# Eight experts on one core: five output stores move from the SyncE queue into GpSimd's queue of loads

## The chip, the core and the metric

The kernel runs on one core of one Trainium2 chip. The metric is the device time of one execution in microseconds (us); before the change the median of five runs is 186.20 us (185.97 to 186.28). The profile used here is one execution of 186.28 us, whose first to last instruction span 184.3 us.

## What is computed

Eight experts, each a two-layer network with its own weights, each on its own 256 rows. All inputs and the output are float32 in device memory.

```python
# n_experts 8, capacity 256, hidden 512, expert_hidden 2048
# x (8,256,512)  w1 (8,512,2048)  w2 (8,2048,512)  b1 (8,2048)  b2 (8,512)
h = np.matmul(x, w1) + b1[:, np.newaxis, :]
h = np.maximum(h, 0)
return (np.matmul(h, w2) + b2[:, np.newaxis, :]).astype(np.float32)
```

The weights are 67.1 MB of the 71.4 MB that the program reads; the output is 4.2 MB.

## The kernel before the change

**Tiles.** Rows of a 128-partition tile are interleaved with the free dimension, so that each partition reads one contiguous run of device memory. The loads issued by GpSimd convert float32 to float16 on the way: `w1sb` and `w2sb` are 128 x 8192 float16 tiles of 2048 KB, `x16` is 256 KB. There are three buffers for w1, three for w2, four for x. The last two w2 are cut: expert 6 comes in two halves (L82), and expert 7 in six pieces with buffers of their own (L90): j 0-4, 4-8, 8-12 (512 KB each), 12-14 (256 KB), and 14-16 in two column halves (128 KB each). They are called p0 to p5 below.

**Stages.** TensorE's work is written out in order. Stage s holds `first_product(s)` (16 values of j, each four matmuls into PSUM at L110 and one relu with bias on ScalarE at L117) and, from s = 3 (LAG), `second_product(s - 3)`: the bias b2 by a one-row matmul (L151), then for every piece of w2, both row blocks and every j one matmul (L163). In the middle of `first_product(e)`, after j = 8, stand the eight transposes of the x of expert e + 1 (L97) with the copy of the result by VectorE (L103). So expert e + 1's x holds up TensorE if it is late, and everything written behind it.

**Stores.** At the end of `second_product(e)`, `store` copies the two PSUM row blocks into an `out` tile, one on VectorE (L130) and one on ScalarE (L131). For experts 0 to 6 one DMA of 512 KB, 4096 bytes to a partition, goes out on SyncE's queue (L137), which has nothing else to do then. For expert 7 each column half is stored in two DMAs of 128 KB, one on SyncE (L134) and one on ScalarE (L135). The `out` tiles have two buffers.

**The order of the loads.** Nearly all loads are GpSimd DMAs and leave in one order: w1(0), b2, w1(1), x(2), w1(2), x(3), w1(3), w2(0), x(4), w1(4), w2(1), x(5), w1(5), w2(2), x(6), w1(6), w2(3), x(7), w1(7), w2(4), w2(5), the halves of w2(6), p0 to p5. `load_x`, `load_w1` and `load_w2` are entries of a list; `issue_until` issues them ahead of the stage that needs them. GpSimd works in order: where a load waits for its buffer (w1(6) for the end of `first_product(3)`, w2(5) for the end of `second_product(2)`), the loads behind it wait too. In the built program a GpSimd DMA also waits for the eighth GpSimd DMA before it, since eight semaphores are used in turn. All DMAs of this queue are called the ring in what follows; the profile names it q0, software_dynamic. SyncE's queue is q1, ScalarE's q10, both hardware_dynamic.

Of the kernel before, what the change touches and what calls it, by code (L numbers as in the profile page):

```python
# [11 lines left out]
def kernel(  # L12
# [9 lines left out]
    nc = tc.nc  # L22
    fp32 = mybir.dt.float32
    fp16 = mybir.dt.float16
    E, T, H = x.shape
    M = w1.shape[2]
    P = 128
    nTB = T // P
    nKC = H // P
    nJ = M // P  # L30
    HH = H // 2
    LAG = 3
    nXF32 = 2

    def ordered(ins):
        return tc.keep_in_program_order(ins)

    singles = ctx.enter_context(tc.tile_pool(name="singles", bufs=1))
    w1_pool = ctx.enter_context(tc.tile_pool(name="w1", bufs=3))
    w2_pool = ctx.enter_context(tc.tile_pool(name="w2", bufs=3))  # L40
    w2t_pool = ctx.enter_context(tc.tile_pool(name="w2t", bufs=1))
    x_pool = ctx.enter_context(tc.tile_pool(name="xp", bufs=4))
    xT_pool = ctx.enter_context(tc.tile_pool(name="xTp", bufs=2))
    hT_pool = ctx.enter_context(tc.tile_pool(name="hT", bufs=LAG + 2))
    out_pool = ctx.enter_context(tc.tile_pool(name="outp", bufs=2))
    psum_x = ctx.enter_context(tc.tile_pool(name="psum_x", bufs=1, space=bass.MemoryType.PSUM))
    psum_h = ctx.enter_context(tc.tile_pool(name="psum_h", bufs=3, space=bass.MemoryType.PSUM))
    psum_o = ctx.enter_context(tc.tile_pool(name="psum_o", bufs=2, space=bass.MemoryType.PSUM))
# [10 lines left out]
    w1_sb = [None] * E  # L59
    w2_sb = [None] * E  # L60
    hT = [None] * E

    def load_x(e):
        x16[e] = x_pool.tile([P, nTB, H], fp16, tag="x16", name="x16")
        ordered(nc.gpsimd.dma_start(  # L65
            out=x16[e], in_=x[e].rearrange("(p tb) h -> p tb h", tb=nTB)
        ))
# [7 lines left out]
    def load_w2(e):  # L75
        src = w2[e].rearrange("(p j) h -> p j h", j=nJ)
        w2_sb[e] = []
        if e < E - 1:
            t = w2_pool.tile([P, nJ, H], fp16, tag="w2", name="w2sb")
            step = nJ if e < E - 2 else nJ // 2  # L80
            for lo in range(0, nJ, step):
                ordered(nc.gpsimd.dma_start(out=t[:, lo : lo + step, :], in_=src[:, lo : lo + step, :]))  # L82
                w2_sb[e].append((lo, lo + step, 0, H, t[:, lo : lo + step, :]))
            return
        for lo, hi, c0, c1 in (
            (0, 4, 0, H), (4, 8, 0, H), (8, 12, 0, H), (12, 14, 0, H),
            (14, 16, 0, HH), (14, 16, HH, H),
        ):
            t = w2t_pool.tile([P, hi - lo, c1 - c0], fp16, tag=f"w2_{lo}_{c0}", name=f"w2_{lo}_{c0}")
            ordered(nc.gpsimd.dma_start(out=t, in_=src[:, lo:hi, c0:c1]))  # L90
            w2_sb[e].append((lo, hi, c0, c1, t))

    def transposes(e):
        pt = psum_x.tile([P, nKC, T], fp16, tag="psx", name="psx")
        for kc in range(nKC):
            for tb in range(nTB):
                ordered(nc.tensor.transpose(  # L97
                    out=pt[:, kc, tb * P : (tb + 1) * P],
                    in_=x16[e][:, tb, :].rearrange("p (q kc) -> p q kc", kc=nKC)[:, :, kc],
                    identity=ident16,  # L100
                ))
        xT[e] = xT_pool.tile([P, nKC, T], fp16, tag="xT", name="xT")
        nc.vector.tensor_copy(out=xT[e], in_=pt)  # L103

    def first_product(e):
        hT[e] = hT_pool.tile([P, nJ, T], fp16, tag="hT", name="hT")
        for j in range(nJ):
            ph = psum_h.tile([P, T], fp32, tag="ph", name="ph")
            for kc in range(nKC):
                ordered(nc.tensor.matmul(  # L110
                    out=ph,
                    lhsT=w1_sb[e][:, kc, :].rearrange("p (q j) -> p q j", j=nJ)[:, :, j],
                    rhs=xT[e][:, kc, :],
                    start=(kc == 0),
                    stop=(kc == nKC - 1),
                ))
            nc.scalar.activation(  # L117
                out=hT[e][:, j, :],
                in_=ph,
                func=mybir.ActivationFunctionType.Relu,  # L120
                bias=b1T[:, j, e : e + 1],
                scale=1.0,
            )
            if j == nJ // 2 and e + 1 < E:
                transposes(e + 1)

    def store(e, po, c0, c1, split):
        w = c1 - c0
        out_sb = out_pool.tile([P, nTB, w], fp32, tag=f"out{w}", name=f"out{w}")
        nc.vector.tensor_copy(out=out_sb[:, 0, :], in_=po[0])  # L130
        nc.scalar.copy(out=out_sb[:, 1, :], in_=po[1])  # L131
        dst = out[e].rearrange("(p tb) h -> p tb h", tb=nTB)[:, :, c0:c1]
        if split:
            nc.sync.dma_start(out=dst[:, 0, :], in_=out_sb[:, 0, :])  # L134
            nc.scalar.dma_start(out=dst[:, 1, :], in_=out_sb[:, 1, :])  # L135
        else:
            nc.sync.dma_start(out=dst, in_=out_sb)  # L137

    def second_product(e):
        if e < E - 1:  # L140
            blocks = [(0, H, psum_o, "po")]
        else:
            blocks = [(0, HH, psum_o, "po"), (HH, H, psum_h, "ph")]
        acc = {}
        for c0, c1, pool, tag in blocks:
            for tb in range(nTB):
                t = pool.tile(
                    [P, c1 - c0], fp32, tag=tag if tag == "ph" else f"{tag}{tb}", name=f"acc{tb}"
                )
                acc[c0, tb] = t  # L150
                ordered(nc.tensor.matmul(  # L151
                    out=t,
                    lhsT=ones1,
                    rhs=b2_sb[0:1, e * H + c0 : e * H + c1],
                    start=True,
                    stop=False,
                ))
        for lo, hi, p0, p1, t in w2_sb[e]:
            mine = [b for b in blocks if p0 <= b[0] and b[1] <= p1]
            for tb in range(nTB):  # L160
                for j in range(lo, hi):
                    for c0, c1, _, _ in mine:
                        ordered(nc.tensor.matmul(  # L163
                            out=acc[c0, tb],
                            lhsT=hT[e][:, j, tb * P : (tb + 1) * P],
                            rhs=t[:, j - lo, c0 - p0 : c1 - p0],
                            start=False,
                            stop=(j == nJ - 1),
                        ))
            if hi == nJ:  # L170
                for c0, c1, _, _ in mine:
                    store(e, [acc[c0, tb] for tb in range(nTB)], c0, c1, e == E - 1)

    x32 = singles.tile([P, nXF32, nTB, H], fp32)
    for e in range(nXF32):
# [4 lines left out]
        out=b2_sb,  # L180
        in_=b2.rearrange("e h -> (e h)").rearrange("(o f) -> o f", o=1),
# [10 lines left out]
    for j in range(nJ):  # L192
        for s in range(2):
            ordered(nc.tensor.matmul(  # L194
                out=pb[s * 64 : (s + 1) * 64, j, :, :],
# [5 lines left out]
    for s in range(2):  # L201
        nc.vector.tensor_copy(  # L202
            out=b1T[s * 64 : (s + 1) * 64, :, :], in_=pb[s * 64 : (s + 1) * 64, :, :, s]
        )
    transposes(0)

    loads = []
    for s in range(1, E + LAG):
        if s < E:
            if s >= nXF32:  # L210
                loads.append((load_x, s))
            loads.append((load_w1, s))
        if s >= LAG:
            loads.append((load_w2, s - LAG))
    n = 0

    def issue_until(done):
        nonlocal n
        while n < len(loads) and not done():
            loads[n][0](loads[n][1])  # L220
            n += 1

    for s in range(E + LAG):
        issue_until(lambda: (
            (min(s + 2, E - 1) < E and w1_sb[min(s + 2, E - 1)] is not None)
            and (s + 2 < LAG or w2_sb[min(s + 2 - LAG, E - 1)] is not None)
        ))
        if s < E:
            first_product(s)
        if s >= LAG:  # L230
            second_product(s - LAG)


# [28 lines left out]
```

## Time and profile before

| | |
|---|---|
| median of five runs | 186.20 us |
| profiled execution | 186.28 us, its span 184.3 us, granted TensorE clock 0.926 |
| TensorE matmul busy | 137.9 us (75%) |
| ScalarE busy | 62.7 us (34%) |
| VectorE / GpSimd busy | 13.5 us / 16.9 us |
| bytes | 71.39 MB read, 4.19 MB written, 410 GB/s over the span |
| stores of experts 0 to 6 | 7 issues, median 9.0 us from issue to landing |
| the same, last two (experts 5 and 6) | issued at 164.0 and 172.0 us, landed 8.1 and 6.6 us later |

How to read it: the span is cut into slices with each engine's busy share in tenths; the DMA row is the mean of the 16 DMA engines. The queues are listed with bytes and with the share of 16 engines' time that their packets took; a load counts there with the float16 bytes that it writes, so its megabytes are half of what it reads. The timeline lists instructions of an engine in order, with the idle time before a group and what ended it. The chain of waits is followed back from the last instruction to what released it.

### The profile page before, as it was taken

The page shows a single profiled execution, that of the slowest core. Times are in us where ns is not written, and L with a number is a line of the kernel's source. Part 1 is how long each engine was busy: PE and PEld are TensorE (multiplying, and loading weights), DVE is VectorE, ACT ScalarE, POOL GpSimd, SP SyncE. Part 2 cuts the span into 40 slices and gives each one's busy share as a digit, 9 for nine tenths or more (in the row PEclk, how much of TensorE's full clock was granted, in tenths as well). Part 3 has the DMA queues.
Part 4 walks back from the last instruction along what each step waited for, and adds up shares of the span by engine and source line. Part 5 has one row for each costly group of instructions (what it writes and reads, how often), then busy time and mean ns, then how long its engine had stood idle before and what let it go on. Part 6 is the DMA issues. An engine that isn't in the chain of part 4 may idle for free.

```text
span 184.3 us, 2209 instructions
## 1 busy us (share of the span) xinstructions
PE 137.9 (75%) x946; PEld 99.1 (54%) x946; DVE 13.5 (7%) x22; ACT 62.7 (34%) x138; POOL 16.9 (9%) x37
## 2 busy tenths in 40 slices
PE   0546969396561999529995499916999996999971
PEld 0534969296551846428465364815648842434750
DVE  0320101001000100001010101001010010101001
ACT  0022869487260513604226060631506901010101
POOL 7100030302100012000110000100006200100000
PEclk9999999999875699965999789995799999999999
DMA  5999999999999999999999999999999999999983
GB/s 198 271 213 194 220 228 224 198 204 229 228 224 199 203 228 228 180 275 220 206 199 243 264 211 217 203 272 232 206 203 224 238 251 206 244 235 254 218 199 114
DMA packets 6488, 40.57 MB, mean 220 GB/s; under 512 B 688, under 2 KB 1728, under 8 KB 4432
## 3 DMA queue, kind: packets, MB, share of 16 engines
q0 software_dynamic: 4320, 35.14, 91.2%
q1 hardware_dynamic: 1568, 4.46, 6.5%
q10 hardware_dynamic: 592, 0.85, 1.3%
q8 instruction: 7, 0.11, 0.2%
q14 instruction: 1, 0.01, 0.0%
HBM read 71.39 MB, written 4.19 MB: 410 GB/s over the span
## 4 chain that ended last, share of the span: by engine, by line
DMA 57%; PE 31%; another core or an unknown queue 5%; POOL 3%; issue 1%; ACT 0%; ACTq 0%; POOLq 0%
DMA x<-in_x_dram 25%; DMA w<-in_w_dram 19%; PE ph L110 16%; DMA w1sb<-in_w_dram 12%; PE acc L163 12%; PE psx L97 2%; PE acc L151 1%; POOL w2sb L82 1%; POOL w L90 1%; POOL w1sb L71 1%; ACT out L131 0%; POOL b_sb L179 0%; POOL ident masks.py:199 0%; ACTq L135 0%
## 5 line engine op out<-in xcount | busy, mean ns | idle before, releaser
L110 PE MATMUL ph<-xT,w1sb 128*128 128x256 f16 x512 | 68.6, 300 | 11.7 <-DMA w1sb<-in_w_dram 11.7
L117 ACT ACTIVATE hT<-ph,b1T 128x256 f16<-128x256 f32 x128 | 57.0, 473 | 47.6 <-PE ph L110 47.5
L110 PEld LDWEIGHTS <-w1sb 128*128 128x128 f16 x512 | 61.8, 149 | 17.9 <-DMA w1sb<-in_w_dram 12.7
L163 PE MATMUL acc<-w2sb,hT 128*128 128x512 f16 x224 | 49.7, 379 | 1.8 <-DMA w2sb<-in_w_dram 1.8
L163 PEld LDWEIGHTS <-hT 128*128 128x128 f16 x288 | 27.5, 98 | 32.2 <-issue 6.8
L131 ACT COPY out<-acc 128x512 f32<-128x512 f32 (+1 forms) x9 | 4.9, 541 | 59.9 <-PE acc L163 59.9
L97 PE MATMUL psx<-ident,x 128*128 128x128 f16 x64 | 7.0, 276 | 21.3 <-DMA x<-in_x_dram 20.6
L97 PEld LDWEIGHTS <-x 128*128 128x128 f16 x64 | 5.6, 132 | 22.3 <-DMA x<-in_x_dram 21.5
L103 DVE COPY xT<-psx 128x1024 f16<-128x1024 f16 x8 | 5.5, 691 | 85.1 <-PE psx L97 85.1
L130 DVE COPY out<-acc 128x512 f32<-128x512 f32 (+1 forms) x9 | 5.7, 632 | 73.5 <-PE acc L163 73.5
L71 POOL DMA_DIRECT2D w1sb<-in_w_dram x8 | 4.4, 553 | 68.0 <-PE ph L110 67.2
L82 POOL DMA_DIRECT2D w2sb<-in_w_dram x8 | 4.3, 536 | 57.1 <-PE acc L163 57.1
L194 PE MATMUL pb<-ident,b_rows 16*64 16x16 f32 x64 | 3.7, 266 | 6.5 <-DMA b_rows<-in_b_dram 6.5
L163 PE MATMUL acc<-w,hT 128*128 128x256 f16 x64 | 7.5, 272 | 1.2 <-DMA w<-in_w_dram 1.2
L194 PEld LDWEIGHTS pb<-ident,b_rows 16*64 16x64 f32 x64 | 3.6, 198 | 6.5 <-issue 6.5
L117 ACT ACT_TABLE_LOAD x1 | 1.3, 1283 | 10.9 <-DVE b1T L202 10.9
L151 PE MATMUL acc<-b_sb,ones 1*128 1x512 f16 (+1 forms) x18 | 4.8, 355 | 0.0
L90 POOL DMA_DIRECT2D w<-in_w_dram x6 | 3.6, 613 | 12.6 <-DMA w2sb<-in_w_dram 12.6
L65 POOL DMA_DIRECT2D x<-in_x_dram x6 | 3.3, 546 | 2.3 <-DMA w1sb<-in_w_dram 2.3
L151 PEld LDWEIGHTS <-ones 1*128 1x128 f16 x18 | 1.1, 93 | 2.1 <-issue 2.1
L189 DVE CAST x<-x 128x1024 f16<-128x1024 f32 x2 | 1.5, 764 | 4.2 <-DMA x<-in_x_dram 4.1
L202 DVE COPY b1T<-pb 64x128 f32<-64x128 f32 x2 | 0.6, 288 | 3.5 <-PE pb L194 3.5
(8 smaller groups left out, 2.0 us busy)
## 6 DMA issues: line engine op xcount, KB each, us to landing
w1sb<-in_w_dram POOLq DMA_DIRECT2D x8, 2048.0 KB, 33.6
w2sb<-in_w_dram POOLq DMA_DIRECT2D x6, 2048.0 KB, 47.3
out_dram<-out SPq DMA_DIRECT2D x7, 512.0 KB, 9.0
w2sb<-in_w_dram POOLq DMA_DIRECT2D x2, 1024.0 KB, 24.5
x<-in_x_dram POOLq DMA_DIRECT2D x6, 256.0 KB, 40.3
w<-in_w_dram POOLq DMA_DIRECT2D x3, 512.0 KB, 32.0
x<-in_x_dram ACTq DMA_DIRECT2D x1, 512.0 KB, 5.3
x<-in_x_dram SPq DMA_DIRECT2D x1, 512.0 KB, 4.4
```

Of the source, the lines that this page charges most:

```text
L71: ordered(nc.gpsimd.dma_start(out=w1_sb[e], in_=w1[e].rearrange("(p kc) m -> p kc m", kc=nKC)))
L82: ordered(nc.gpsimd.dma_start(out=t[:, lo : lo + step, :], in_=src[:, lo : lo + step, :]))
L90: ordered(nc.gpsimd.dma_start(out=t, in_=src[:, lo:hi, c0:c1]))
L97: ordered(nc.tensor.transpose(out=pt[:, kc, tb * P : (tb + 1) * P], in_=x16[e][:, tb, :].rearrange("p (q kc) -> p q kc", kc=nKC)[:, :, kc] ...
L103: nc.vector.tensor_copy(out=xT[e], in_=pt)
L110: ordered(nc.tensor.matmul(out=ph, lhsT=w1_sb[e][:, kc, :].rearrange("p (q j) -> p q j", j=nJ)[:, :, j], rhs=xT[e][:, kc, :], start=(kc == 0),
L117: nc.scalar.activation(out=hT[e][:, j, :], in_=ph, func=mybir.ActivationFunctionType.Relu, bias=b1T[:, j, e : e + 1], scale=1.0,)
L130: nc.vector.tensor_copy(out=out_sb[:, 0, :], in_=po[0])
L131: nc.scalar.copy(out=out_sb[:, 1, :], in_=po[1])
L151: ordered(nc.tensor.matmul(out=t, lhsT=ones1, rhs=b2_sb[0:1, e * H + c0 : e * H + c1], start=True, stop=False,))
L163: ordered(nc.tensor.matmul(out=acc[c0, tb], lhsT=hT[e][:, j, tb * P : (tb + 1) * P], rhs=t[:, j - lo, c0 - p0 : c1 - p0], start=False, sto ...
L194: ordered(nc.tensor.matmul(out=pb[s * 64 : (s + 1) * 64, j, :, :], lhsT=b1_rows.rearrange("r (q j) -> r q j", j=nJ)[:, :, j], rhs=ident[0 ...
```

## The change

Experts 0 to 4 no longer store on SyncE's queue. `store` puts the DMA by (`pending`), and `flush` issues it on GpSimd, at a set place in the list of loads, which now carries the earliest stage with each entry: flush(0) stands behind w2(3), flush(1) behind w2(4), flush(2) behind w2(5), flush(3) behind the halves of w2(6), and flush(4) between p0 and p1. Experts 5 and 6 still store on SyncE, expert 7 on SyncE and ScalarE. The `out` tiles of 512 columns have three buffers where they had two, and the two of expert 7 have their own. The loads keep their order among themselves, and TensorE, VectorE and ScalarE keep theirs. In the built program GpSimd issues 34 DMAs where it issued 29, and SyncE four stores where it issued nine.

```diff
+    RING = 4
-    out_pool = ctx.enter_context(tc.tile_pool(name="outp", bufs=2))
+    out_pool = ctx.enter_context(tc.tile_pool(name="outp", bufs=3))
+    pending = {}
...
-        for lo, hi, c0, c1 in (
-            (0, 4, 0, H), (4, 8, 0, H), (8, 12, 0, H), (12, 14, 0, H),
-            (14, 16, 0, HH), (14, 16, HH, H),
-        ):
-            t = w2t_pool.tile([P, hi - lo, c1 - c0], fp16, tag=f"w2_{lo}_{c0}", name=f"w2_{lo}_{c0}")
-            ordered(nc.gpsimd.dma_start(out=t, in_=src[:, lo:hi, c0:c1]))
-            w2_sb[e].append((lo, hi, c0, c1, t))
+    def load_w2_piece(e, lo, hi, c0, c1):
+        t = w2t_pool.tile([P, hi - lo, c1 - c0], fp16, tag=f"w2_{lo}_{c0}", name=f"w2_{lo}_{c0}")
+        src = w2[e].rearrange("(p j) h -> p j h", j=nJ)
+        ordered(nc.gpsimd.dma_start(out=t, in_=src[:, lo:hi, c0:c1]))
...
+    def flush(e):
+        dst, src = pending.pop(e)
+        ordered(nc.gpsimd.dma_start(out=dst, in_=src))
+
     def store(e, po, c0, c1, split):
         w = c1 - c0
-        out_sb = out_pool.tile([P, nTB, w], fp32, tag=f"out{w}", name=f"out{w}")
+        pool = out_pool if w == H else singles
+        out_sb = pool.tile([P, nTB, w], fp32, tag=f"out{c0}_{w}", name=f"out{w}")
...
+        elif e <= RING:
+            pending[e] = (dst, out_sb)
         else:
             nc.sync.dma_start(out=dst, in_=out_sb)
...
+    ring = []
+    for s in range(1, E + LAG - 1):
         if s < E:
             if s >= nXF32:
-                loads.append((load_x, s))
-            loads.append((load_w1, s))
+                ring.append((s - 2, load_x, (s,)))
+            ring.append((s - 2, load_w1, (s,)))
         if s >= LAG:
-            loads.append((load_w2, s - LAG))
...
+            ring.append((s - 2, load_w2, (s - LAG,)))
+        if s >= 2 * LAG:
+            ring.append((s - 2, flush, (s - 2 * LAG,)))
+    e = E - LAG - 1
+    for piece in (
+        (0, 4, 0, H), (4, 8, 0, H), (8, 12, 0, H), (12, 14, 0, H),
+        (14, 16, 0, HH), (14, 16, HH, H),
+    ):
+        ring.append((0, load_w2_piece, (E - 1,) + piece))
+        if e <= RING:
+            ring.append((e + LAG + 1, flush, (e,)))
+            e += 1
 
     for s in range(E + LAG):
...
+        while ring and ring[0][0] <= s:
+            _, put, args = ring.pop(0)
+            put(*args)
```

More of the change, by code (lines that the diff above doesn't have):

```diff
@@ L77, in load_w2 @@
         w2_sb[e] = []
[L78 to L84, printed above, removed]
-        for lo, hi, c0, c1 in (
-            (0, 4, 0, H), (4, 8, 0, H), (8, 12, 0, H), (12, 14, 0, H),
-            (14, 16, 0, HH), (14, 16, HH, H),
-        ):
-            t = w2t_pool.tile([P, hi - lo, c1 - c0], fp16, tag=f"w2_{lo}_{c0}", name=f"w2_{lo}_{c0}")
-            ordered(nc.gpsimd.dma_start(out=t, in_=src[:, lo:hi, c0:c1]))
-            w2_sb[e].append((lo, hi, c0, c1, t))
+        t = w2_pool.tile([P, nJ, H], fp16, tag="w2", name="w2sb")
+        step = nJ if e < E - 2 else nJ // 2
+        for lo in range(0, nJ, step):
+            ordered(nc.gpsimd.dma_start(out=t[:, lo : lo + step, :], in_=src[:, lo : lo + step, :]))
+            w2_sb[e].append((lo, lo + step, 0, H, t[:, lo : lo + step, :]))
+    def load_w2_piece(e, lo, hi, c0, c1):
+        t = w2t_pool.tile([P, hi - lo, c1 - c0], fp16, tag=f"w2_{lo}_{c0}", name=f"w2_{lo}_{c0}")
+        src = w2[e].rearrange("(p j) h -> p j h", j=nJ)
+        ordered(nc.gpsimd.dma_start(out=t, in_=src[:, lo:hi, c0:c1]))
+        if w2_sb[e] is None:
+            w2_sb[e] = []
+        w2_sb[e].append((lo, hi, c0, c1, t))
     def transposes(e):
@@ L205 @@
     transposes(0)
-    loads = []
-    for s in range(1, E + LAG):
+    ring = []
+    for s in range(1, E + LAG - 1):
         if s < E:
             if s >= nXF32:
-                loads.append((load_x, s))
-            loads.append((load_w1, s))
+                ring.append((s - 2, load_x, (s,)))
+            ring.append((s - 2, load_w1, (s,)))
         if s >= LAG:
-            loads.append((load_w2, s - LAG))
[L215 to L221, printed above, removed]
+            ring.append((s - 2, load_w2, (s - LAG,)))
[10 more added lines that the diff above has]
+            e += 1
     for s in range(E + LAG):
[L224 to L227, printed above, removed]
+        while ring and ring[0][0] <= s:
+            _, put, args = ring.pop(0)
+            put(*args)
         if s < E:
@@ L231 @@
             second_product(s - LAG)
+    assert not ring and not pending
 _INS = ['x', 'w1', 'w2', 'b1', 'b2']
```

## The prediction

> **What bounds the kernel now.** I read the slices of the page and its list of queues first, then TensorE's timeline, the chain of waits, and the DMA queues in windows.
>
> ```profile
> DMA  5999999999999999999999999999999999999983
> ...
> q0 software_dynamic: 4320, 35.14, 91.2%
> q1 hardware_dynamic: 1568, 4.46, 6.5%
> ```
>
> The DMA engines are nine tenths busy or more from the second slice (of 4.6 us) to the 38th, q0 (the ring) with 91.2% of their time, SyncE's queue with 6.5%. No stretch is empty that a load could be pulled into. TensorE is fed by the ring; its timeline, each row with start, time, and idle time before it:
>
> ```profile
> 26.09 4.15 PE L110 MATMUL ph<-xT,w1sb 128*128 128x256 f16 x36 [1.40 <-DMA w1sb<-in_w_dram]
> ...
> 37.01 4.15 PE L110 MATMUL ph<-xT,w1sb 128*128 128x256 f16 x36 [3.26 <-DMA w1sb<-in_w_dram]
> ...
> 58.99 1.04 PE L97 MATMUL psx<-ident,x 128*128 128x128 f16 x8 [5.09 <-DMA x<-in_x_dram]
> ...
> 81.97 1.04 PE L97 MATMUL psx<-ident,x 128*128 128x128 f16 x8 [5.93 <-DMA x<-in_x_dram]
> ...
> 103.91 1.04 PE L97 MATMUL psx<-ident,x 128*128 128x128 f16 x8 [4.44 <-DMA x<-in_x_dram]
> ...
> 125.85 1.04 PE L97 MATMUL psx<-ident,x 128*128 128x128 f16 x8 [5.15 <-DMA x<-in_x_dram]
> ...
> 156.22 7.07 PE L163 MATMUL acc<-w2sb,hT 128*128 128x512 f16 x32 [1.49 <-DMA w2sb<-in_w_dram]
> ...
> 167.67 3.61 PE L163 MATMUL acc<-w2sb,hT 128*128 128x512 f16 x16 [0.29 <-DMA w2sb<-in_w_dram]
> ...
> 176.15 1.91 PE L163 MATMUL acc<-w,hT 128*128 128x256 f16 x16 [0.73 <-DMA w<-in_w_dram]
> 178.53 1.94 PE L163 MATMUL acc<-w,hT 128*128 128x256 f16 x16 [0.47 <-DMA w<-in_w_dram]
> ```
>
> A row that waits for a DMA dates that DMA's landing. The last two rows are p2 (16 matmuls) and p3 to p5 (8, 4, 4). The chain of waits ends:
>
> ```profile
> 142.56 35.93 DMA w<-in_w_dram
> 178.48 0.04 issue
> 178.53 1.48 PE acc L163 x12
> 180.01 0.02 issue
> 180.03 0.38 ACT out L131
> ```
>
> So p3's landing at 178.48 sets the end, then 12 matmuls, then ScalarE and the last stores, 184.3 − 180.01 = 4.3 us, which the change leaves alone.
>
> **Two prices.** Between 26.09 and 37.01 the ring brought one w1 and one x, 2304 KB in 10.92 us: 211 KB per us. So 512 KB (p0, p1, p2 each) takes 2.43 us, 256 KB (p3) 1.21. From x(5) to x(6), 81.97 to 103.91, and from x(6) to x(7), 103.91 to 125.85, are 21.94 us each; a w1, a w2 and an x are 4352 KB or 20.63 us; the 1.31 left over is one store. From x(4) to x(5), 58.99 to 81.97, it is 22.98, so the first store cost 2.35. The window 72 to 82 gives that store 13.8% of 10 us, 1.38 us of packets; the other 1 us is load packets that ran slow, once.
>
> **The change, part by part.**
> *Bytes.* None are added or removed. Before, all seven stores pass ahead of p3's landing; after, five stand ahead of p3 in the ring, and the two of SyncE come earlier than now. If a store costs the ring what it costs beside it, p3 lands at 178.48 again: 0 us.
>
> *The price of a ring store* is not shown. The nearest rows are 1.31 and 2.35 for one on SyncE's queue, 1.21 for 256 KB of x in the ring, whose float32 bytes are a store's, 512 KB. Bounds: 0 (it hides wholly) makes 5 x −1.31 = −6.6 us, 2.35 each makes 5 x 1.04 = +5.2. I take 1.31, by the two regular stores and the near 1.21; at 1.21 it would be −0.5. Three rows lie within 0.1 of each other, so neither far end is in the range. The single excess of 1 us I let recur, at the first ring store or the first SyncE store; if it stays away, −1.0.
>
> The Trainium skill ("DMA: Bandwidth & Descriptors", Anatomy of one DMA) gives a GpSimd DMA a fixed cost of about 2.0 us, most of it the receipt of the last write, worst to device memory. Charged to the ring five times, an estimate by that page, it would be +10 us. The row that bears on it: the ring's 29 DMAs run with the DMA engines at nine tenths throughout, so that cost lies beside other packets in this trace, though no store is among them.
>
> *Instructions on GpSimd.* Five more issues of 0.55 us (the row of x loads: 3.3 us for 6), beside waits of 67.2 us (w1) and 57.1 us (w2): nothing, for the loads behind them wait 20 to 50 us in the ring. Of their waits, flush(0) to flush(3) follow w2 loads that already wait for the `second_product` that makes the output. For flush(0): w2(3) issued at 72.41, the output is ready at 72.74. New is flush(4): GpSimd reaches it at about 140, expert 4's output is ready at about 152, and p1 to p5 wait behind it. The ring then still holds flush(2), w2(6), flush(3), p0 and flush(4), 1.3 + 9.7 + 1.3 + 2.4 + 1.3 = 16 us: hidden, while that output is less than 16 us late. The wait for the eighth DMA back makes p5 follow w2(6)'s second half (165) with p0 to p4 and two stores, some 12 us, in front: hidden too. If not, each us of empty ring is 1 us of time.
>
> *Third buffer.* out(6) waits for flush(3), which follows w2(6) in the ring (about 165.1 + 1.3 + 1.3 for a SyncE store between, 167.7); ScalarE needs it at about 168.7. One us of cover; without it only store 6 is late, which costs nothing.
>
> *What comes sooner.* The stores are later, so the loads are earlier. Ahead of w2(5) lay stores 0 to 3, now flush(0) and flush(1): two fewer, 2.6 us, so landing 153.6 for 156.2. Ahead of w2(6)'s end lay 0 to 4, now flush(0) to flush(2): 165.1 for 167.67. x(7) comes at 123.2 for 125.85, and TensorE's work to 154.2 shifts with it. So TensorE ends `second_product(6)` 2.6 us earlier, and SyncE issues store 6 at 169.4 instead of 172.0. The loads after that give the 2.6 us back: flush(3) and flush(4) now stand before p1.
>
> *The tail.* Where did store 6 go before? The window 175 to 178.5:
>
> ```profile
> q0 software_dynamic: 493, 0.34, 64.3%
> q1 hardware_dynamic: 144, 0.52, 39.7%
> ```
>
> All its 0.52 MB, 1.39 us of packets, ran there, 3.0 us after its issue, and so between the landings of p2 and p3: 178.48 − 176.1 is 2.4 us, where p3 alone takes 1.21. This gap let TensorE finish p2 (1.91 us) with 0.47 to spare. After, store 6 runs from 169.4 + 3.0 = 172.4 to about 176, beside p1 and the first part of p2. p3 still lands at 178.48, by the sum of bytes, but p2 then lands 1.21 before it, at 177.27, not at 176.1. TensorE starts p2 at 177.32, ends at 179.23, and does the 12 matmuls behind it without a wait: 179.23 + 1.48 = 180.71 for 180.01. **+0.70 us**: TensorE, not p3, is then the last to wait for.
>
> The Trainium skill (same page, "Issuing engines are not separate DMA queues") says that moving a DMA to another queue saves only issue time, since all run on the same 16 engines; that alone would make 0, 186.3 us. For the bytes the row of slices agrees; the order at the tail is what it leaves out.
>
> **Sum.** 186.28 + 0.70 = 186.98 for an execution like the profiled one; this stood 0.08 above the median of the runs, so 186.9.
>
> **Rivals.**
> 1. *Nothing moves* (186.2, 185.8 to 186.5). Store 6 still falls between p2 and p3. For: stores on SyncE's queue took 8 to 15 us to land in the middle of the run. Against: the last two took 8.1 and 6.6, and 169.4 + 8.1 is 177.5. It decides when half the store, 0.6 us, lies behind p2.
> 2. *Faster* (185.4, 184.4 to 185.8). Ring stores are cheaper than SyncE's: the slow load packets at the first store do not recur (−1.0), or each store costs 1.21 (−0.5); with the +0.7 of the tail, 186.2 − 1.5 + 0.7 = 185.4. The hope that earlier loads alone end earlier is worth at most TensorE's waits of 1.49 and 0.29, to 184.4, but p3's landing speaks against it. For: the 2.35 beside 1.31. Against: the later stores showed no such excess, so there is at most one to save.
> 3. *Much slower* (188.5 to 195). A store in the ring holds the loads behind it until its write is confirmed. The last 128 KB stores took 2.1 us from issue to landing, and their bytes take 0.3: 1.8 x 5 = 9.0, +0.7 = 195.9 if all of it holds the ring; a quarter makes 188.9. For: such a wait would be beside the ring before, inside it after. Against: no gap behind any load in the slices. It decides from a hold of 0.1 us per store.
>
> **How the numbers follow.** My forecast 0.47, rival 1 0.25, rival 2 0.20, rival 3 0.08. About 0.2%, 0.37 us, is what can be told from no change: 185.8 to 186.6. Faster 0.20 is rival 2; the same 0.25 is rival 1; slower 0.55 is my forecast and rival 3. The likeliest case alone spans 186.5 to 187.4 (half of store 6 behind p2 to one more excess of a half us); the range takes in rival 1 and the edge of rivals 2 and 3: 185.7 to 187.8.
>
> **What would show it.** Right: in TensorE's timeline the matmuls of `second_product(5)` start near 153.6, p2 near 177.3, and p3 to p5 follow without a wait for a DMA; store 6 is issued near 169.4; the queue shares keep 98% in sum; the chain ends in more matmuls than 12. Wrong: p3 waits for a DMA again (rival 1), p3 lands under 178 (rival 2), slices under nine tenths or a store's share in the ring above 1.4 us (rival 3). An idle DMA engine between 141 and 170 would say that flush(4) starved the ring.

## The result, and the profile after

Median 186.30 us over 23 runs (186.12 to 187.06) beside 186.04 us over 44 runs of the kernel before: ratio 1.0022, 95% interval 1.0015 to 1.0029. The change costs 0.3 us by the medians and 0.4 by the ratio; the forecast was a cost of 0.7. The 23 runs fall into two groups, 14 from 186.12 to 186.36 and 9 from 186.58 to 187.06; those of the kernel before show no such gap. The profiled execution took 186.30 us, its span is 184.5 us.

From the page of the changed kernel, the slices of the DMA engines and the queues:

```profile
DMA  5998999999999999998999989999999999999973
...
q0 software_dynamic: 5040, 37.76, 94.6%
q1 hardware_dynamic: 848, 1.84, 2.8%
```

Five stores of 0.52 MB have gone from q1 to q0; the packet time of the two is 97.4% of the span where it was 97.7%. No stretch has run empty. TensorE's timeline in the changed kernel (start, time, in brackets the idle time before the row and what ended it):

```profile
122.93 1.04 PE L98 MATMUL psx<-ident,x 128*128 128x128 f16 x8 [7.33 <-DMA x<-in_x_dram]
...
153.22 8.75 PE L171 MATMUL acc<-w2sb,hT 128*128 128x512 f16 x32 [2.19 <-DMA w2sb<-in_w_dram]
...
172.90 1.91 PE L171 MATMUL acc<-w,hT 128*128 128x256 f16 x16 [0.99 <-DMA w<-in_w_dram]
176.03 3.82 PE L171 MATMUL acc<-w,hT 128*128 128x256 f16 x32 [1.22 <-DMA w<-in_w_dram]
```

x(7) comes at 122.93 for 125.85, w2(5) at 153.2 for 156.2. The last row holds p2 to p5 in one: TensorE waits for p2 and for nothing behind it. The chain of waits says the same, with 28 matmuls behind the DMA of p2 where 12 stood behind p3:

```profile
153.46 22.53 DMA w<-in_w_dram
175.99 0.04 issue
176.03 3.35 PE acc L171 x28
179.38 0.02 issue
179.40 0.38 ACT out L137
```

But ScalarE's copy starts at 179.40, 0.63 us *earlier* than before (180.03), and the span is 0.2 us longer. What is lost lies behind it, where no engine computes. Two views show it. In them a drain is one of an engine's closing instructions, and a slot is one of the eight semaphores that the DMAs of SyncE and ScalarE use in turn. SyncE's own waits at the end, first of the kernel before, then of the changed one (total, times, longest):

```profile
SPq L257 <- DMA out_dram<-out: 1.9, 4, 1.0
```

```profile
SPq L271 <- DMA out_dram<-out: 2.1, 1, 2.1
```

Before the program ends, SyncE waits for the semaphores of all DMA queues, two to an instruction, in a fixed order of slots. Before, four of these waits were spread over the landings; after, the wait for the first slot holds until the last landing and the others follow it. And the end itself, before and after (operation, count, durations, first and last start):

```profile
L257 SPq DRAIN  x3: 7/7/7, 183.5 to 183.8; - x3
...
L257 POOLq EVENT_SEMAPHORE_RANGE_CLEAR  x1: 141/141/141, 183.9 to 183.9; - x1
```

```profile
L271 SPq DRAIN  x3: 7/7/7, 183.2 to 183.5; - x3
...
L271 POOLq EVENT_SEMAPHORE_RANGE_CLEAR  x1: 139/139/139, 184.1 to 184.1; - x1
```

SyncE's drain, which says that all DMAs are done, comes 0.3 us earlier than before, and GpSimd's clearing of the semaphores 0.2 us later: GpSimd's own drain ahead of it starts at 183.81, 0.45 us after the wait before it, where it was 0.08 us. In that last stretch the changed kernel has one packet on the instruction queue, the kernel before none (queues in the window 183 to 186: packets, MB, share):

```profile
q14 instruction: 1, 0.01, 1.0%
```

It starts at 184.52, where the span ends, 0.7 us behind that drain.

The table gathers what the semaphore and packet records of every profile give; us from the span's start. SyncE's drain is the second of its three, 0.06 us behind the first, and the last column runs from its start to the end of the execution (device time less that start).

| kernel | p2 | p3 | p5 | ScalarE's first store | last landing | SyncE's drain | to the end |
|---|---|---|---|---|---|---|---|
| before | 176.11 | 178.48 | 179.82 | 180.43 | 183.30 | 183.56 | 2.72 |
| changed | 175.99 | 177.85 | 179.21 | 179.81 | 182.67 | 183.25 | 3.05 |
| changed, again | 176.51 | 177.77 | 179.12 | 180.21 | 183.07 | 183.65 | 3.04 |
| before, 3 tiny loads | 175.79 | 177.27 | 179.71 | 180.15 | 183.03 | 183.60 | 2.72 |
| changed, 7 tiny loads | 175.98 | 177.71 | 179.01 | 179.67 | 182.54 | 182.68 | 3.07 |
| before, 5 tiny ring loads | 175.81 | 177.54 | 179.72 | 180.14 | 183.05 | 183.31 | 3.04 |
| changed, store 4 behind p2 | 174.97 | 177.72 | 179.07 | 179.67 | 182.53 | 183.11 | 3.04 |
| before, 16 memsets | 175.53 | 177.02 | 179.45 | 179.89 | 182.75 | 183.01 | 2.54 |
| changed, 16 memsets | 175.97 | 177.83 | 179.19 | 179.79 | 182.65 | 183.22 | 2.54 |
| changed, all three edits | 175.21 | 178.00 | 179.31 | 179.95 | 182.82 | 182.96 | 2.54 |
| three buffers alone | 176.17 | 178.38 | 179.69 | 180.34 | 183.20 | 183.46 | 2.71 |
| 5 and 6 behind p5 | 174.07 | 175.30 | 176.70 | 177.77 | 180.66 | 180.80 | 2.58 |
| 4, 5 and 6 behind p5 | 172.80 | 174.01 | 175.45 | 176.50 | 180.55 | 180.69 | 2.58 |
| 0 to 4 on SyncE, 5 and 6 behind p5 | 174.32 | 175.53 | 176.97 | 178.21 | 181.08 | 181.46 | 2.93 |

From the first two rows: −0.62 to ScalarE's store, +0.31 from there to SyncE's drain (3.13 to 3.44), +0.33 behind it: +0.02, as the two executions differ (186.28, 186.30). What this pair hides is said under "Sum".

### The profile page after: what moved, and what is told of

The parts are those of the page before. It is cut to its first block, busy times and chain, and to the rows that moved or that the text cites. A ratio compares the mean times of both kernels' runs of the same rounds, so it can differ in the third digit from the quotient of the medians.

```text
span 184.5 us, 2204 instructions
## 1 busy us (share of the span) xinstructions
PE 138.4 (75%) x946; PEld 98.8 (54%) x946; DVE 13.4 (7%) x22; ACT 62.7 (34%) x138; POOL 19.6 (11%) x42
## 4 chain that ended last, share of the span: by engine, by line
DMA 71%; PE 14%; issue 8%; another core or an unknown queue 2%; POOL 2%; ACT 0%; ACTq 0%; POOLq 0%
DMA x<-in_x_dram 24%; DMA w2sb<-in_w_dram 22%; DMA w1sb<-in_w_dram 12%; DMA w<-in_w_dram 12%; PE ph L111 7%; PE acc L171 6%; PE psx L98 1%; POOL w2sb L83 1%; POOL w1sb L73 1%; ACT out L137 0%; POOL out_dram L130 0%; PE acc L159 0%; POOL b_sb L187 0%; POOL ident masks.py:199 0%
## 5 line engine op out<-in xcount | busy, mean ns | idle before, releaser
L111 PE MATMUL ph<-xT,w1sb 128*128 128x256 f16 x512 | 67.8, 298 | 8.8 <-DMA w1sb<-in_w_dram 8.8
L171 PE MATMUL acc<-w2sb,hT 128*128 128x512 f16 x224 | 51.2, 389 | 2.2 <-DMA w2sb<-in_w_dram 2.2
L171 PEld LDWEIGHTS <-hT 128*128 128x128 f16 x288 | 28.0, 99 | 34.8 <-issue 10.2
L130 POOL DMA_DIRECT2D out_dram<-out x5 | 2.7, 538 | 18.3 <-ACT out L137 13.1
```

Of the source, the lines that this page charges most:

```text
L111: ordered(nc.tensor.matmul(out=ph, lhsT=w1_sb[e][:, kc, :].rearrange("p (q j) -> p q j", j=nJ)[:, :, j], rhs=xT[e][:, kc, :], start=(kc == 0),
L171: ordered(nc.tensor.matmul(out=acc[c0, tb], lhsT=hT[e][:, j, tb * P : (tb + 1) * P], rhs=t[:, j - lo, c0 - p0 : c1 - p0], start=False, sto ...
```

## The experiments

Each was timed beside the kernel before on the same chip. "Tiny" loads are 64 bytes that nothing reads.

**The changed kernel once more**, for a second profile.

> The changed kernel once more, for a second profile. Theory: three parts add up to the change. (a) p5 lands about 0.6 us earlier than before, since a store packet takes 159 ns in the ring and mostly 172 ns on SyncE's queue; (b) the end behind the last landing is 0.8 us longer: SyncE's waits begin with the semaphore that lands last (+0.3) and GpSimd's last drain starts 0.45 us after its release instead of 0.08 (+0.5); (c) the tail costs 0 to 0.7 us, depending on how far store 6 lies ahead of p2. So the ends of (b) come again, and the run is 186.1 to 187.1 us. Rival (the whole loss is the tail): the end behind the last landing is as before, 1.0 us.

Measured: 186.72 us median, both groups again (4 runs from 186.12 to 186.33, 8 from 186.68 to 186.94), 1.0022 (1.0010 to 1.0034). This profile caught the long kind, 186.69 us. TensorE's timeline in it:

```profile
153.14 7.07 PE L171 MATMUL acc<-w2sb,hT 128*128 128x512 f16 x32 [1.28 <-DMA w2sb<-in_w_dram]
...
173.16 1.91 PE L171 MATMUL acc<-w,hT 128*128 128x256 f16 x16 [2.12 <-DMA w<-in_w_dram]
176.55 3.65 PE L171 MATMUL acc<-w,hT 128*128 128x256 f16 x32 [1.48 <-DMA w<-in_w_dram]
```

`second_product(5)` takes 7.07 us, not 8.75, TensorE is done sooner, and SyncE issues store 6 at 168.44 instead of 170.21. It lands at 176.0, ahead of p2; p2 and p3 land 1.26 us apart, the time of p3 alone, and the work behind p2 sets the end: ScalarE's store at 180.21, 0.4 us later than in the other profile. What made the 8.75 is the granted clock. The window 153 to 162 in the first profile and in this one (busy time of each engine, then the granted TensorE clock, the DMA share and GB/s):

```profile
153.00:162.00 9.00, 8.78 (x33) 3.56 (x33) 0.69 (x1) 0.00 (x0) 1.77 (x3) 0.81 1.05 227
```

```profile
153.00:162.00 9.00, 8.86 (x41) 3.75 (x41) 0.69 (x1) 0.58 (x1) 2.13 (x4) 1.00 1.05 227
```

0.81 against 1.00. A slower TensorE made the shorter execution: it sent store 6 off so late that 58 of its 128 packets ran behind the last packet of p2 (all 128 in the profile of the kernel before, none in this one). Point (c) holds; the ends of (b) come again.

**The slot of the last store, in the kernel before.**

```diff
     nc.scalar.dma_start(out=b1_rows, in_=b1.rearrange("e (s i) -> (e s) i", s=2))
+    tiny = singles.tile([1, 3, 16], fp32)
+    for i in range(3):
+        nc.sync.dma_start(out=tiny[:, i, :], in_=b1[0:1, 0:16])
```

> The kernel before with three loads of 64 bytes on SyncE's queue at the start that nothing reads. They move the semaphore of the last store from the sixth of eight slots to the first, as the change did. Theory: SyncE, which waits for the semaphores two at an instruction and in slot order, stands at the first slot until the last landing and then walks through all the others: 0.58 us from the last landing to its drain instead of 0.26, so +0.3 us (186.3 to 186.4 beside 186.05). Rival (the order of the waits costs nothing): 0, within 0.1 us.

Measured: 186.37 us, 1.0014 (1.0001 to 1.0027). From the last landing to SyncE's drain 0.57 us for 0.26 (table), and one wait where there were four:

```profile
SPq L260 <- DMA out_dram<-out: 2.0, 1, 2.0
```

The walk, SyncE's remaining waits behind the last landing, is real, and has nothing to do with where the stores went: only with how many hardware DMAs the program issues.

**The same in the changed kernel**, seven tiny loads in place of three.

> The changed kernel with seven loads of 64 bytes on SyncE's queue at the start that nothing reads. They move the semaphore of the last store from the first slot to the eighth. Theory: SyncE's walk behind the last landing shrinks from 0.58 to about 0.15 us, so -0.4 us against the changed kernel, to about 185.9 to 186.0. Rival (the walk costs nothing, the loss is the tail alone): no change, 186.3 to 186.5.

Measured: 186.43 us, 1.0005 (0.9993 to 1.0017); both groups, 4 runs from 185.75 to 185.95 and 8 from 186.29 to 186.77, each 0.3 to 0.4 us under its like in the changed kernel. From last landing to drain 0.14 us for 0.58. As expected; the median hides it, since more runs fell into the long group.

**Five more DMAs in the ring, in the kernel before.**

```diff
+    tiny = singles.tile([1, 5, 16], fp32)
+    def load_tiny(i):
+        ordered(nc.gpsimd.dma_start(out=tiny[:, i, :], in_=b1[0:1, 0:16]))
...
         if s >= LAG:
             loads.append((load_w2, s - LAG))
+        if 2 * LAG <= s < 2 * LAG + 4:
+            loads.append((load_tiny, s - 2 * LAG))
...
             w2_sb[e].append((lo, hi, c0, c1, t))
+            if lo == 0:
+                load_tiny(4)
```

> The kernel before with five loads of 64 bytes in the ring at the places where the change has its five stores; nothing reads them, and the stores stay on SyncE's queue. Theory: the longer stretch between GpSimd's release and its last drain, 0.45 us instead of 0.08, comes from the number of GpSimd's instructions, so it appears here too: +0.4 to +0.5 us, 186.5. Rival: it comes from stores in the ring, or from chance, and this kernel takes 186.0 to 186.1.

Measured: 186.44 us, 1.0013 (1.0003 to 1.0022). The pause between release and drain that the theory was about did not appear (0.08 us); but the end takes 3.04 us from SyncE's drain, as in the changed kernel, with the same instruction packet, here 1.1 us behind the span's last instruction. So 0.3 us come with a longer GpSimd program, though not at the place expected, and no store in the ring is needed for it.

**The store of expert 4 behind p2.**

```diff
-        if e <= RING:
+        if piece[0] == 8:
             ring.append((e + LAG + 1, flush, (e,)))
             e += 1
```

> The changed kernel with the store of expert 4 one place further on: between p2 and p3 instead of p0 and p1. Bytes and ends are the same. Theory of the tail (the end is decided by p2 where nothing lies between p2 and p3): p2 lands 1.2 us earlier, p3 where it was (177.8), so TensorE's last 12 matmuls hang on p3 again: ScalarE's first store is issued at 179.8 in every execution, and the executions of 186.6 to 187.1 us are gone: median 186.2 to 186.3. Rival (the longer executions come from the clock or from the ring alone): both kinds of execution stay, median as the changed kernel's, 186.3 to 186.7.

Measured: 186.15 us, all 11 runs from 185.94 to 186.35, 1.0006 (0.9998 to 1.0015). TensorE's timeline:

```profile
175.01 1.91 PE L171 MATMUL acc<-w,hT 128*128 128x256 f16 x16 [1.61 <-DMA w<-in_w_dram]
177.76 1.95 PE L171 MATMUL acc<-w,hT 128*128 128x256 f16 x16 [0.84 <-DMA w<-in_w_dram]
```

TensorE waits for p3 again, and the long executions are gone, although store 6 went out early (168.46). The same bytes in another order, at full clock: the tail theory is shown.

**16 memsets on GpSimd, in the kernel before.**

```diff
     nc.vector.memset(ones1, 1.0)
+    spare = singles.tile([P, 16, 16], fp32)
+    for i in range(16):
+        ordered(nc.gpsimd.memset(spare[:, i, :], 0.0))
```

> The kernel before with 16 small memsets on GpSimd at its start that nothing reads; no DMA is added. Theory (GpSimd's longer program has one more block of instructions to fetch, which shows as one instruction packet of 8192 bytes at the end): the same packet appears, and from SyncE's drain to the end of the execution there are 3.04 us, as in the changed kernel, not 2.72: +0.3 us, 186.4. Rival (it is the number of ring DMAs): no such packet, 2.72 us, 186.1.

Measured: 185.88 us, 0.9987 (0.9976 to 0.9998): faster, against theory and rival. The packet came, but in mid-run, at 144.6; the queues in the window 143 to 146:

```profile
q14 instruction: 1, 0.01, 0.6%
```

The end shrank to 2.54 us. This gave a new theory: the length of GpSimd's program matters through where it crosses from one block of instructions to the next.

**The same memsets in the changed kernel.**

> The changed kernel with 16 small memsets on GpSimd at its start that nothing reads. The memsets on the kernel before gave neither what my theory nor what its rival expected: an instruction packet of 8192 bytes came, but at 144.6 us, in mid-run, and the end became shorter (2.54 us from SyncE's drain to the end of the execution, for 2.72). New theory: it matters where GpSimd's program passes from one block of instructions to the next; at the very end, as in the changed kernel, the fetch is waited for, in mid-run it is hidden. So here the packet comes in mid-run, GpSimd's last drain starts 0.08 us after its release, and the end takes 2.55 us for 3.04: 0.5 us less than the changed kernel, 185.7 (short tail) or 186.2 (long tail). Rival (stores in the ring make the drain wait): 0.44 us before the drain and 3.04 us again, 186.3 or 186.7.

Measured: 185.81 us, 0.9987 (0.9976 to 0.9999), packet at 119.0, GpSimd's last drain 0.08 us after its release, end 2.54 us. Both groups are there again (8 runs from 185.47 to 185.95, 3 from 186.13 to 186.42), each 0.5 us under its like in the changed kernel. The new theory's numbers hold and its rival falls: with this alone the changed kernel is slightly faster than the kernel before.

**All three edits** (store 4 behind p2, seven tiny loads, 16 memsets).

> The changed kernel with all three edits: store of expert 4 between p2 and p3, seven 64-byte loads that nothing reads, 16 memsets that nothing reads. Theory (the three losses are separate and add up): 186.15 of the run with the late store, less 0.44 (walk), less 0.5 (end of GpSimd) is 185.2 us, 0.9 under the kernel before: what five cheaper stores in the ring, landing p5 0.65 us earlier, are worth without the rest, and the better end. Rival (they are not separate): 185.6 or over.

Measured (5 runs): 185.50 us, 0.9969 (0.9957 to 0.9981), between theory and rival. Walk (0.14) and end (2.54) are as expected; p3 landed at 178.00 for 177.72, which makes the 0.3 that lacks. Why the ring was later is open.

**Three buffers alone.** RING = −1, no entries for `flush` in the list.

> The changed kernel's three output buffers and its list, but all stores on SyncE's queue at once, as before. Theory: buffers are worth nothing, 186.05 within 0.2 us, p5 lands at 179.7 to 179.8. Rival (the third buffer, not the queue, lands p5 earlier): p5 at 179.1.

Measured: 186.12 us, 0.9998 (0.9990 to 1.0007), p5 at 179.69. The buffers are worth nothing.

**Experts 5 and 6 in the ring behind p5.**

```diff
-    RING = 4
+    RING = 6
...
-        if e <= RING:
+        if piece[0] == 0 and e < 5:
             ring.append((e + LAG + 1, flush, (e,)))
             e += 1
+    for e in range(5, RING + 1):
+        ring.append((e + LAG + 1, flush, (e,)))
```

> The changed kernel with the stores of experts 5 and 6 in the ring too, behind p5. Theory: two stores of 1.2 to 1.3 us no longer stand ahead of p3, so p3 lands near 175.4 and p2 near 174.1, TensorE's last matmuls end 1.9 us earlier, and the two stores run under the tail; with seven hardware DMAs the last store holds the seventh of eight slots, 0.4 us off SyncE's walk: 186.5 - 1.9 - 0.4 = 184.2 us, at most 185.0 if the last stores have to queue behind the two. Rival (the DMA bytes bind whatever their order): 186.0 and over.

Measured (4 runs): 183.39 us, 0.9858 (0.9845 to 0.9872). The chain of waits in it:

```profile
153.51 20.56 DMA w<-in_w_dram
174.07 0.04 issue
174.12 3.23 PE acc L171 x28
```

p2 lands at 174.07 as expected, 1.92 us before the changed kernel's. The two stores run from 176.7 to 179.2, while TensorE, ScalarE and the last stores finish. Of the rest, to 183.4 for 184.2, 0.5 us is the end: this program's instruction packet falls into mid-run (at 171.7), and the end takes 2.58 us for 3.05. The expectation had also begun at 186.5, 0.2 us above the profiled execution.

**Expert 4 behind p5 as well.** The same with `e < 4` and `range(4, RING + 1)`.

> As the run with the stores of experts 5 and 6 behind p5, and that of expert 4 behind it too. Theory: p3 lands another 1.2 us earlier, but now the ring's own end, near 179.2 plus its landing, comes close to the landing of the last stores: 183.3 to 184.3 us. Rival (bytes bind): 186.0 and over; if the last stores queue behind 3.7 us of ring stores, it is slower than the run with two.

Measured (4 runs): 183.18 us, 0.9849 (0.9836 to 0.9863). p2 lands another 1.27 us earlier, but the last landing only 0.11: the last stores, issued 1.27 us earlier, now run beside the end of the ring (its last store lands at 179.2) and take 3.3 us from issue to landing for 2.1. Here the bytes bind.

**Experts 0 to 4 on SyncE, 5 and 6 behind p5.**

```diff
-        elif e <= RING:
+        elif 5 <= e <= RING:
```

(and no `flush` entries for 0 to 4)

> Stores of experts 0 to 4 on SyncE's queue as before, those of experts 5 and 6 in the ring behind p5. Theory: moving the last two gains 1.9 to 2.5 us here too, and the five stores on SyncE's queue cost the 0.65 us that they save in the ring: p5 lands at 177.3 for 176.7, and the last ring store at 179.8 for 179.2; about 184.0 to 184.5 us, also with a walk of 0.4 us over four semaphores. Rival (the queue of the first five doesn't matter): p5 at 176.7, 183.4 to 183.8.

Measured: 186.01 us median, 184.39 to 186.23, 0.9974 (0.9955 to 0.9993). A miss. The profile caught the fastest run, and p5 landed at 176.97, between theory and rival. TensorE's timeline:

```profile
155.90 7.07 PE L171 MATMUL acc<-w2sb,hT 128*128 128x512 f16 x32 [2.34 <-DMA w2sb<-in_w_dram]
...
171.05 7.16 PE L171 MATMUL acc<-w,hT 128*128 128x256 f16 x64
```

Stores on SyncE go ahead of loads, so w2(5) lands at 155.9 instead of 153.2, and from then on TensorE waits for nothing: it sets the end. Seven of the 12 runs took 185.97 us or more; that those are the ones in which the clock fell to half in this stretch (which made `second_product(5)` 1.7 us longer in other profiles) is likely, but none of them was profiled. So the ring stores of the change do buy something, 2.7 us of room for TensorE, which is worth nothing until the tail is free.

## Why the prediction was right or wrong

**The tail: right in mechanism, and it happens in part of the runs.** The prediction said that store 6 would be issued at 169.4, pass ahead of p2, and leave p2 to land 1.21 us before p3, with TensorE as the last to wait for. The second profile has 168.44 and 1.26 us; the chain ends in 28 matmuls as foreseen:

```profile
176.55 3.23 PE acc L171 x28
```

Moving one store behind p2 removes the effect. But the term was mis-sized. ScalarE's first store follows p3's landing by 1.95 us in the kernel before and by 2.44 in the second profile: 0.49, not 0.70, since the 28 matmuls in a row took 3.23 us and not 1.91 + 1.48. And the step took `second_product(5)` as 7.07 us. In the first profile it took 8.75, with part of it at half clock, store 6 went at 170.21 and nearly half of it stayed between p2 and p3 (1.86 us apart), where the prediction's own first rival drew the line; there the tail cost nothing. The two other profiles of short executions (seven tiny loads, 16 memsets) have the half clock in that stretch and 0.01 us of tail too. That the runs without a profile divide into their two groups in this way is likely, not shown.

**p3 lands at 178.48 again: wrong by 0.6 us.** The term that failed is the price of a ring store, taken as that of a store on SyncE's queue, 1.31. A store's packet of 4096 bytes took 159 ns in 569 of 637 ring packets, and 172 ns in 807 of 896 on SyncE's queue before, and 77 to 90% of them in the other profiles with seven stores there (counts from the packet records). Eight packets to a DMA engine and store, 10 ns on the average, five stores: 0.4 us. p5 landed at 179.45 to 179.82 in the five profiles with seven stores on SyncE and at 179.01 to 179.31 in the six with five in the ring, 0.53 us apart on the average. The slow load packets at the first store, which I let recur, did recur, at 115.6 to 118.4 us, just ahead of the first ring store. Their sum differs, though: 0.39 to 0.80 us per DMA engine in the five profiles, 0.14 to 0.55 in the six, 0.2 less on the average, so a part of the 0.53 may be theirs and not the queue's. With experts 5 and 6 behind p5 in both, the comparison gave only 0.27 us, from one profile each, which differ by as much in slow packets. That p5 lands earlier is shown; how much of it is the price of a packet is open.

**"4.3 us, which the change leaves alone": wrong, and the step that holds the loss.** From the last matmul that counts to the span's end it became 184.52 − 179.38 = 5.14 us. Two parts, neither of them in any step: SyncE's walk, +0.3, since nine hardware DMAs in place of fourteen put the last store on the first of eight slots; and GpSimd's end, +0.3 in the execution (+0.5 in the span), which comes with a longer GpSimd program whose instruction packet falls on the very end. Each was produced in the kernel before without moving a store, and taken out of the changed kernel without moving one back. That GpSimd waits for this packet is not shown: its late drain stands 0.7 us ahead of the packet, and in the run with five tiny ring loads, where the end was as long, that drain was not late at all.

**Sum.** −0.6 (p3) +0.3 (walk) +0.3 (GpSimd) is 0.0 for the pair of profiles, and +0.4 with the long tail; the measured cost is 0.3 to 0.4. The pair hides a cost, since the profile of the kernel before has full clock in the stretch from 153 to 162 and that of the changed kernel has not. The kernel before has executions of both kinds too. Its profile, then that of its run with three tiny loads, in the same columns as above:

```profile
153.00:162.00 9.00, 7.51 (x35) 3.19 (x34) 0.69 (x1) 0.58 (x1) 0.71 (x1) 1.00 0.99 230
```

```profile
153.00:162.00 9.00, 6.63 (x23) 2.58 (x23) 0.51 (x1) 0.59 (x1) 0.71 (x1) 0.81 1.03 239
...
172.86 7.49 PE L163 MATMUL acc<-w,hT 128*128 128x256 f16 x64
```

In the second kind p2 and p3 are in time and TensorE sets the end. Like beside like, by ScalarE's first store: at full clock 180.34 and 180.43 with seven stores on SyncE's queue, 180.21 with the change; at half clock 179.89 to 180.15, and 179.67 to 179.81. So the change gains 0.2 to 0.3 us there, loses 0.6 behind it, and costs 0.3 to 0.5, which fits the measured 0.3 to 0.4. One profile alone stands for the changed kernel at full clock.

**Which step failed.** The forecast had one term, the tail, at +0.70 in every execution. The runs showed 0.49 of it in the one profile that has it, nothing in three others, and 0.6 us that p3 gains, so up to ScalarE's store the change is a gain. The loss is the 0.6 us behind it, in the 4.3 us that the prediction left alone. The forecast's sign came out right by luck: the term that decided it was not in the sum.

**Rivals.** That store 6 still falls between p2 and p3 (rival 1) is half true of the short runs. That the loads end earlier with the stores in the ring (rival 2) is real, 0.3 to 0.6 us at p5, but the slow first packets recur. No hold of the ring behind a store (rival 3) appeared: the loads behind the stores land on time, and the DMA slices stay full. (A quarter of that hold makes 189.2 by the rival's own terms, 186.2 + 2.25 + 0.7, and not 188.9.) The estimate from the Trainium skill ("DMA: Bandwidth & Descriptors", Anatomy of one DMA) of 2.0 us to a DMA, charged to the ring, is not borne out by any run here: five stores made the ring 0.5 us shorter. GpSimd's wait for expert 4's output (13.1 us) and the eighth-back waits were hidden, as worked out.

## What to carry to other kernels

In a kernel that is bound by its DMA queues, which queue a store takes was worth tenths of a microsecond here; which bytes stand ahead of the last load that matters was worth microseconds. Stores that nothing waits for belong behind the last load, where they run under the last products. On top of the five moves, two more stores there brought the kernel from 186.30 to 183.39 us (186.07 before any move; ScalarE's first store came 2.04 us earlier for the two, and about 0.9 us went at the end, 0.4 in the walk and 0.5 in GpSimd's end). A third brought it to 183.18, where the queue's own end binds. Without the five moves the same two left 7 of 12 runs at 186 us, likely since TensorE then got w2(5) 2.7 us later. And compare what follows the last store too: the order of the final waits and the length of an engine's program moved the end by 0.3 us each.

## What the runs showed of the hardware

- The end of the program depends on which semaphore slot holds the last DMA: 0.14 us from its landing to SyncE's drain in the seventh and the eighth, 0.26 in the sixth, 0.38 in the fourth, 0.57 to 0.58 in the first.
- Queue 14 has a packet of 8192 bytes of instructions at 45 to 48 us in every profile, and with a longer GpSimd program a second one, the earlier the longer the program. Where this second one falls goes with the length of the end: 2.93 to 3.07 us in the six profiles that have it behind 183 us, 2.54 to 2.58 in the five that have it between 118 and 172. 16 memsets that do nothing made either kernel 0.2 to 0.5 us faster. The Trainium skill ("Runtime: NRT & Kernel Launch", Instruction fetch mechanics) calls the cost of crossing a boundary of 16 KiB "mostly hidden"; with the packet in mid-run the profiles agree, and with it at the end they show the longer time. Why a program with no such packet, as the kernel before, takes 2.72 us and not 2.54, no run tells.
- The TensorE clock, halved for 3.4 us somewhere between 153 and 161 us in 6 of 14 profiles, made the changed kernel faster by delaying a store (186.30 us beside 186.69).
- Once in each profile, from 3 us before the first store's packets to 2 us behind their start, 13 to 31 load packets run up to 0.9 us long, 0.1 to 0.8 us per DMA engine in all, whichever queue has the store. The cause is open.
